# Attention values in a hybrid backbone block: V once in 64 columns of the array, even heads in one half of the columns, odd heads in the other

## The chip, the cores and the metric

The kernel runs on one core of a Trainium2 chip. The metric is the time of one execution on the device in microseconds (us), taken as the median of several runs. The profile is that of one execution; its times are microseconds from its first instruction.

The engines are called PE (matrix products and turns), PEld (the loading of PE's stationary operand), DVE, ACT, POOL (element-wise engines) and SP (here: the queue that issues the loads from memory).

## What is computed

Two layers over 512 latent tokens of width 1024, with 256 context tokens. Each layer is a half-step gated FFN, a token mixer, and a second half-step FFN, all with modulation and normalisation around them. The mixer of the first layer is windowed attention with 16 query heads in 4 groups, one key head and one value head of width 64 for each group. A block of 128 queries sees its own and the neighbouring blocks of keys, all context keys, and a sink logit for each head. The part that matters here:

```python
p = jax.nn.softmax(jnp.concatenate([s_win, s_ctx, sinks], axis=-1), axis=-1).astype(v.dtype)
o = (jnp.einsum('bhgqk,bkhd->bqhgd', p[..., :SPAN], v_b)
     + jnp.einsum('bhgqk,bkhd->bqhgd', p[..., SPAN:SPAN + C_], vc))
```

The mixer of the second layer is a Fourier mixing. All data are float32.

## The kernel before

Weight products are made of three products of rounded float32 parts (`mm3`): weights are loaded (`wr`), cut on ACT (`wh`) and DVE (`wl`), and multiplied. The products of the attention weights with V are plain float32 products.

The stages follow each other: a head, the first FFN over latent tokens, the one over context tokens, the attention (`attention`), its output product (`project` with `attn_wo`), the second FFN, the second layer. Attention first makes K, V and Q in six groups of products (`group`). `kv_post` adds the bias, turns K, and has ACT copy V from `kvb` into a tile of its own, where each value head stands twice side by side: 64 columns and the same 64 columns once more, so that the stationary operand of a value product has 128 columns.

The core of the attention is a loop over 16 steps, a step being a group g and a block b of 128 queries (`steps`). A step has four heads. The order of the instructions on PE, and within the loop on DVE and ACT too, is the order of the program (`pin`). Step n does this:

- `weights_turned(n)`: PE turns the finished attention weights p of the four heads, key tile by key tile (4 key tiles for the first and last block, 5 for the others), into banks `pt`; ACT copies each bank to `pT`, 128 keys by 512 columns (4 heads by 128 queries).
- `scores(n+2)`: PE makes the scores of the step after next into banks `s` (one bank for each head with 4 key tiles, two with 5). DVE adds the mask and takes the running minimum (`nm`), ACT takes the exponentials, DVE adds the sums, takes the reciprocal and scales p.
- In steps 3 to 6 PE turns a part of Q (`q_flip`, banks `qt`), and ACT copies it. From step 7 on, weights of the following output product are gated on DVE and cut on ACT and DVE in between (`gate_next`, `weights`).
- `values(n)`: PE multiplies V by `pT`, one product for each key tile, summed in one bank `o`. Its 128 rows hold the 64 values twice; its 512 columns hold the four heads. From the upper half of the rows ACT copies the even heads to `oT[g]`, from the lower half the odd heads: two copies of 64 rows by 2 heads by 128 queries.

PE has eight banks, given out in the order in which the program asks for them. A bank is free again when its reader has emptied it: ACT for `pt`, `qt` and `o`, DVE for `s`.

After the core, `project` splits `oT` (`uh` on ACT, `ul` on DVE) and PE multiplies it by the cut weights (`y`).

All instructions go through one helper, so that they have the same line, L68, in the profile; they are told apart by the names of their tiles.

Of the kernel before, what the change touches and what calls it, by code (L numbers as in the profile page):

```python
# [10 lines left out]
F32 = mybir.dt.float32  # L11
# [4 lines left out]
P = 128  # L16
# [13 lines left out]
KVH = 4  # L30
GRP = HEADS // KVH
HD = 64
# [68 lines left out]
class Emitter:  # L101
# [33 lines left out]
    def mm(self, out, lhsT, rhs, start, stop):  # L135
        self.nc.tensor.matmul(out, lhsT, rhs, start=start, stop=stop)
# [734 lines left out]
    def attention(self, w_kv, w_q, w_ao, h1, ch, rest):  # L871
        nc = self.nc
        ins = self.ins
        sync = nc.sync
        mm = self.mm
# [13 lines left out]
        V = []  # L889

        def kv_post(tp, ps):
            V.append(self.slot([P, 2, KVH, 2 * HD], F32, "V"))
            kv = self.slot([P, 2, 512], F32, "kvb")
            for tt in range(2):
                nc.vector.tensor_tensor(kv[:, tt], ps[:, tt * 512 : (tt + 1) * 512], bkv, ALU.add)
            kks = []
            for tt in range(2):
                t = 2 * tp + tt
                kr = kv[:, tt, :256]
                if t < NT:  # L900
                    kr = self.rope(kr, tabs[:, 0, t], tabs[:, 1, t], KVH, nc.vector)
                kk2 = self.slot([P, 2, KVH, 2, HD], F32, "kk2")
                k4 = kr.rearrange("p (h d) -> p h d", d=HD)
                for r in range(2):
                    nc.scalar.copy(kk2[:, 0, :, r].bitcast(F32R), k4)
                for r in range(2):
                    nc.vector.tensor_tensor(kk2[:, 1, :, r], k4, kk2[:, 0, :, r], ALU.subtract)
                kks.append(kk2)
            for tt in range(2):
                v4 = kv[:, tt, 256:512].rearrange("p (h d) -> p h d", d=HD).unsqueeze(2)  # L910
                nc.scalar.copy(
                    V[tp][:, tt].rearrange("p h (r d) -> p h r d", r=2), v4.broadcast_to([P, KVH, 2, HD])
                )
            return tp, kks

        def kv_flip(tp, kks, tt):
# [77 lines left out]
        nc.pin(True)  # L994
        ps = group(0, w_kv)
        k0 = kv_post(0, ps)
        flip()
        ps = group(1, w_kv, between=lambda: kv_flip(*k0, 0))
        kv_flip(*k0, 1)
        k1 = kv_post(1, ps)  # L1000
        ps = group(2, w_kv, last=True, between=lambda: kv_flip(*k1, 0))
        kv_flip(*k1, 1)
        bq = self.slot([P, D], F32, "bq")
        sync.dma_start(bq, ins["b_qkv"][:, :D].broadcast_to([P, D]))
        k2 = kv_post(2, ps)
        ps = group(0, w_q[0], between=lambda: kv_flip(*k2, 0))
        kv_flip(*k2, 1)
# [12 lines left out]
        oT = []  # L1020
# [72 lines left out]
        def values(g, b, keys, pT):  # L1093
            nk = len(keys)
            o = self.bank("o")
            for i, kt in enumerate(keys):
                mm(o, V[kt // 2][:, kt % 2, g], pT[i], start=(i == 0), stop=(i == nk - 1))
            tok = slice(b * P, (b + 1) * P)
            for r in range(2):
                rs = slice(r * HD, (r + 1) * HD)  # L1100
                src = o[rs].rearrange("p (c r q) -> p c r q", c=2, r=2)[:, :, r]
                nc.scalar.copy(oT[g][rs, :, tok], src)

        steps = [(g, b) for g in range(KVH) for b in range(NT)]
        oT.append(self.slot([P, 2, SEQ], F32, "oT"))
# [5 lines left out]
        for n, (g, b) in enumerate(steps):  # L1111
            fetch = n >= CORE_FETCH and self.n_split < w_ao + CORE_TILES
            if fetch:
                self.gate_next()
            t = weights_turned(*due.pop(0))
            if b == 0 and g > 0:
                oT.append(self.slot([P, 2, SEQ], F32, "oT"))
            if n + 2 < len(steps):
                due.append(scores(*steps[n + 2]))
            if Q_TURN <= n < Q_TURN + 4:  # L1120
                q_flip(*(q01 if n < Q_TURN + 2 else q11), (n - Q_TURN) % 2)
            if fetch:
                self.weights(self.n_split, ahead=0)
            values(*t)
            if n == 0:
                q11 = q_bias(1, 1, ps1)
                for i in range(4):
                    q_rope(*(q01 if i < 2 else q11), i % 2, nc.gpsimd)
            if Q_TURN - 1 <= n < Q_TURN + 3:
                q_parts(*(q01 if n < Q_TURN + 1 else q11), (n + 1 - Q_TURN) % 2)  # L1130
# [208 lines left out]
```

## Time and profile before

| | us |
|---|---|
| median of three runs | 2053.14 (2052.12 to 2055.15) |
| the profiled execution | 2051.99 |
| its span, first to last instruction | 2050.0 |
| PE busy | 2004.1 |
| weight loads of PE busy | 1684.2 |
| DVE busy | 1324.0 |
| ACT busy | 714.5 |
| the attention core | from about 676 to 811 |

Busy times are shares of the span of one engine each and overlap. A matmul's record in the profile lasts longer than the distance to the next one, since matmuls run in a pipeline; the distance of the starts, or the chain of waits, tells how fast they follow each other. The chain of waits goes back from the last instruction, at each step to what released it or to the instruction before it on its engine.

### The profile page before, as it was taken

The page shows a single profiled execution, that of the slowest core. Times are in us where ns is not written, and L with a number is a line of the kernel's source. Part 1 is how long each engine was busy: PE and PEld are TensorE (multiplying, and loading weights), DVE is VectorE, ACT ScalarE, POOL GpSimd, SP SyncE. Part 2 cuts the span into 40 slices and gives each one's busy share as a digit, 9 for nine tenths or more (in the row PEclk, how much of TensorE's full clock was granted, in tenths as well). Part 3 has the DMA queues.
Part 4 walks back from the last instruction along what each step waited for, and adds up shares of the span by engine and source line. Part 5 has one row for each costly group of instructions (what it writes and reads, how often), then busy time and mean ns, then how long its engine had stood idle before and what let it go on. Part 6 is the DMA issues. An engine that isn't in the chain of part 4 may idle for free.

```text
span 2050.0 us, 25222 instructions
## 1 busy us (share of the span) xinstructions
PE 2004.1 (98%) x9990; PEld 1684.2 (82%) x9990; DVE 1324.0 (65%) x1888; ACT 714.5 (35%) x1090; POOL 50.6 (2%) x56
## 2 busy tenths in 40 slices
PE   6999999999999999999999999999999699999998
PEld 5788888899888776888888888888888688888887
DVE  7659985698756887566558545765764873322754
ACT  3322233433634688322224322222432452222420
POOL 3000000000000300000000000000000000000000
PEclk9999999999999999999999999999999899999999
DMA  9656533387712012365543325654340323332321
GB/s 364 234 197 204 195 125 124 119 314 275 258 48 71 1 42 83 103 225 195 187 164 113 123 95 194 213 196 134 113 144 3 133 92 103 104 102 83 119 76 41
DMA packets 81910, 292.56 MB, mean 143 GB/s; under 512 B 9856, under 2 KB 10112, under 8 KB 81792
## 3 DMA queue, kind: packets, MB, share of 16 engines
q1 hardware_dynamic: 81792, 290.96, 41.4%
q8 instruction: 78, 1.28, 0.3%
q14 instruction: 40, 0.33, 0.0%
HBM read 288.83 MB, written 2.10 MB: 142 GB/s over the span
## 4 chain that ended last, share of the span: by engine, by line
PE 94%; DVE 4%; ACT 1%; issue 0%; DMA 0%; SPq 0%; DVEq 0%; ACTq 0%
PE up L68 52%; PE y L68 31%; PE qkv L68 4%; PE o L68 3%; PE s L68 1%; PE pt L68 1%; DVE acc L68 1%; PE tp L68 1%; DVE p L68 1%; DVE x L68 1%; PE ab L68 0%; PE qt L68 0%; DVE wr L68 0%; DMA wr<-in_wi_head_dram 0%; PE gp L68 0%
## 5 line engine op out<-in xcount | busy, mean ns | idle before, releaser
L68 DVE TENSOR_TENSOR wl<-wr,wh 128x1024 fp32r<-128x1024 f32 x356 | 426.0, 1219 | 108.4 <-ACT wh L68 74.0
L68 ACT CAST wh<-wr 128x1024 fp32r<-128x1024 f32 (+1 forms) x364 | 367.6, 1046 | 189.9 <-PE y L68 85.6
L68 PE MATMUL up<-hh,wh 128*128 128x512 f32 (+1 forms) x1152 | 429.4, 373 | 0.0
L68 PE MATMUL up<-hl,wh 128*128 128x512 f32 (+1 forms) x1152 | 427.9, 371 | 0.0
L68 PE MATMUL up<-hh,wl 128*128 128x512 f32 (+1 forms) x1152 | 427.8, 371 | 0.0
L68 PE MATMUL y<-wh,uh 128*128 128x512 f32 x920 | 303.8, 392 | 13.2 <-ACT X L68 13.2
L68 ACT ACTIVATE sg<-up 128x512 f32<-128x512 f32 (+1 forms) x110 | 61.1, 556 | 715.3 <-PE up L68 715.3
L68 PE MATMUL y<-wh,ul 128*128 128x512 f32 x920 | 302.6, 390 | 0.1
L68 PE MATMUL y<-wl,uh 128*128 128x512 f32 x920 | 302.3, 390 | 0.0
L68 DVE TENSOR_TENSOR u<-up,sg 128x512 f32<-128x512 f32 (+1 forms) x110 | 70.0, 637 | 354.1 <-PE up L68 353.8
L68 PEld LDWEIGHTS up<-hl,wh 128*128 128x128 f32 x1152 | 217.0, 188 | 37.5
L68 PEld LDWEIGHTS up<-hh,wl 128*128 128x128 f32 x1152 | 217.1, 188 | 37.2
L68 PEld LDWEIGHTS up<-hh,wh 128*128 128x128 f32 x1152 | 217.1, 188 | 36.9
L68 PEld LDWEIGHTS y<-wh,uh 128*128 128x128 f32 x920 | 173.4, 189 | 49.5 <-ACT uh L68 13.8
L68 PEld LDWEIGHTS y<-wh,ul 128*128 128x128 f32 x920 | 173.2, 188 | 36.6 <-DVE ul L68 0.6
L68 PEld LDWEIGHTS y<-wl,uh 128*128 128x128 f32 x920 | 173.3, 188 | 35.8
L68 DVE SCALAR_TENSOR_TENSOR acc<-mr,silu_c,acc 128x1024 f32<-128x1024 f32 x147 | 186.0, 1279 | 1.4
L68 PE MATMUL up<-h0h,wh 128*128 128x512 f32 x352 | 139.5, 396 | 3.0 <-ACT h0h L68 3.0
L68 DVE TENSOR_TENSOR wr<-wr,gr 128x1024 f32<-128x1024 f32 x104 | 124.5, 1219 | 22.3 <-DMA wr<-in_wo_dram 20.2
L68 PE MATMUL up<-h0l,wh 128*128 128x512 f32 x352 | 138.3, 393 | 0.0
L68 PE MATMUL up<-h0h,wl 128*128 128x512 f32 x352 | 138.1, 392 | 0.0
L68 DVE SCALAR_TENSOR_TENSOR z<-x,y 128x512 f32<-128x512 f32 x48 | 32.7, 682 | 125.1 <-PE y L68 125.0
(158 smaller groups left out, 2290.7 us busy)
## 6 DMA issues: line engine op xcount, KB each, us to landing
wr<-in_wi_dram SPq DMA_DIRECT2D x213, 512.0 KB, 4.4
mr<-in_mod_w_dram SPq DMA_DIRECT2D x144, 512.0 KB, 4.2
wr<-in_wo_dram SPq DMA_DIRECT2D x110, 512.0 KB, 3.6
m<-in_mod_head_dram SPq DMA_DIRECT2D x16, 512.0 KB, 8.0
wr<-in_wqkv_dram SPq DMA_DIRECT2D x12, 512.0 KB, 3.7
wr<-in_attn_wo_dram SPq DMA_DIRECT2D x8, 512.0 KB, 3.5
wr<-in_fourier_wo_dram SPq DMA_DIRECT2D x8, 512.0 KB, 5.4
wr<-in_wi_head_dram SPq DMA_DIRECT2D x8, 448.0 KB, 9.2
```

The source lines that it names most:

```text
L68: ins = f(*args, **kw)
```

## The change

V is copied once, to 64 columns a head. Each key tile gets two products in place of one: the stationary operand is the same 64 columns of V, the moving operand is the 256 columns of the even heads or of the odd heads, and the result goes to the upper 64 or to the lower 64 rows of the bank, 256 columns wide. ACT then copies the bank to `oT` with one instruction over 128 rows in place of two over 64.

```diff
         def kv_post(tp, ps):
-            V.append(self.slot([P, 2, KVH, 2 * HD], F32, "V"))
+            V.append(self.slot([P, 2, KVH, HD], F32, "V"))
...
             for tt in range(2):
-                v4 = kv[:, tt, 256:512].rearrange("p (h d) -> p h d", d=HD).unsqueeze(2)
-                nc.scalar.copy(
-                    V[tp][:, tt].rearrange("p h (r d) -> p h r d", r=2), v4.broadcast_to([P, KVH, 2, HD])
-                )
+                nc.scalar.copy(V[tp][:, tt], kv[:, tt, 256:512].rearrange("p (h d) -> p h d", d=HD))
...
             o = self.bank("o")
             for i, kt in enumerate(keys):
-                mm(o, V[kt // 2][:, kt % 2, g], pT[i], start=(i == 0), stop=(i == nk - 1))
+                heads = pT[i].rearrange("p (c r q) -> p c r q", c=2, r=2)
+                for r in range(2):
+                    mm(
+                        o[r * HD : (r + 1) * HD, : 2 * P].rearrange("p (c q) -> p c q", c=2),
+                        V[kt // 2][:, kt % 2, g], heads[:, :, r], start=(i == 0), stop=(i == nk - 1),
+                    )
             tok = slice(b * P, (b + 1) * P)
-            for r in range(2):
-                rs = slice(r * HD, (r + 1) * HD)
-                src = o[rs].rearrange("p (c r q) -> p c r q", c=2, r=2)[:, :, r]
-                nc.scalar.copy(oT[g][rs, :, tok], src)
+            nc.scalar.copy(oT[g][:, :, tok], o[:, : 2 * P].rearrange("p (c q) -> p c q", c=2))
```

## Rows read from the trace of the kernel before

**Rows 1.** The page: span, and busy time of each engine with its share.
```profile
span 2050.0 us, 25222 instructions
...
PE 2004.1 (98%) x9990; PEld 1684.2 (82%) x9990; DVE 1324.0 (65%) x1888; ACT 714.5 (35%) x1090; POOL 50.6 (2%) x56
```

**Rows 2.** Busy time by stretch: length, engines (instructions), granted clock, DMA share, GB/s.
```profile
600.00:626.00 26.00, 26.00 (x132) 21.83 (x131) 15.63 (x32) 17.53 (x42) 0.00 (x0) 1.00 0.38 122
...
690.00:740.00 50.00, 50.00 (x280) 36.31 (x279) 42.06 (x131) 40.60 (x106) 6.67 (x7) 1.00 0.04 11
740.00:799.00 59.00, 57.03 (x292) 39.58 (x292) 55.31 (x173) 48.89 (x120) 0.00 (x0) 1.00 0.14 44
799.00:811.00 12.00, 11.87 (x51) 6.98 (x50) 2.85 (x4) 8.29 (x16) 0.00 (x0) 1.00 0.54 183
```

**Rows 3.** DVE's waits, 676 to 811: who, for whom, total, times, longest.
```profile
DVE wl L68 <- ACT wh L68: 9.1, 1, 9.1
DVE p L68 <- PE s L68: 7.3, 4, 2.6
```

**Rows 4.** DVE's timeline, rows with waits: start, length, instruction, [idle before, releaser].
```profile
678.16 0.62 DVE L68 CUSTOM_DVE_ANT_0 p<-s,mask,nsink 128x384 f32<-128x384 f32 x1 [1.49 <-PE s L68]
...
705.00 0.62 DVE L68 CUSTOM_DVE_ANT_0 p<-s,mask,nsink 128x384 f32<-128x384 f32 x1 [1.11 <-PE s L68]
...
731.66 0.75 DVE L68 CUSTOM_DVE_ANT_0 p<-s,mask,nsink 128x512 f32<-128x512 f32 x1 [2.57 <-PE s L68]
...
740.36 0.62 DVE L68 CUSTOM_DVE_ANT_0 p<-s,mask,nsink 128x384 f32<-128x384 f32 x1 [2.15 <-PE s L68]
```

**Rows 5.** Instructions at tile o: ns min/median/max, first and last start, form.
```profile
L68 PEld LDWEIGHTS o<-pT,V x144: 186/190/192, 680.0 to 808.7; 128*128 128x128 f32 x144
L68 PE MATMUL o<-pT,V x144: 590/592/697, 680.0 to 809.2; 128*128 128x512 f32 x144
L68 ACT COPY oT<-o x32: 350/367/373, 685.0 to 810.2; 64x256 f32<-64x256 f32 x32
```

**Rows 6.** The chain of waits: start, length, what, how many.
```profile
690.19 4.29 PE o L68 x10
694.48 2.18 PE pt L68 x20
```

**Rows 7.** Timeline of the weight loads, from scores to values.
```profile
698.29 0.31 PEld L68 LDWEIGHTS o<-pT,V 128*128 128x128 f32 x2
698.84 0.19 PEld L68 LDWEIGHTS o<-pT,V 128*128 128x128 f32 x1 [0.24 <-issue]
```

**Rows 8.** ACT's groups, 560 to 676: busy us, mean ns, idle before.
```profile
L68 ACT COPY V<-kvb 128x512 f32<-128x512 f32 x6 | 3.4, 616 | 0.0
...
L68 ACT CAST K<-kt 128x256 fp32r<-128x256 f32 x16 | 4.8, 385 | 5.4 <-PE kt L68 5.4
```

**Rows 9.** Timeline of SP's queue: the first load of the output weights.
```profile
731.12 0.33 SPq L164 DMA_DIRECT2D wr<-in_attn_wo_dram  x1
```

**Rows 10.** Timelines of ACT, DVE and PE at the core's end.
```profile
798.14 0.75 ACT L68 COPY oT<-o 64x256 f32<-64x256 f32 x2 [0.19 <-PE o L68]
798.91 2.54 ACT L68 COPY pT<-pt 128x512 f32<-128x512 f32 x5
...
805.39 2.05 ACT L68 COPY pT<-pt 128x512 f32<-128x512 f32 x4
807.31 1.08 ACT L68 CAST wh<-wr 128x1024 fp32r<-128x1024 f32 x1
...
809.56 1.22 DVE L68 TENSOR_TENSOR ul<-oT,uh 128x1024 fp32r<-128x1024 f32 x1
...
810.83 0.73 PE L68 MATMUL y<-wh,ul 128*128 128x512 f32 x2
```

**Rows 11.** PE's wait before 688.38; busy time by stretch, as rows 2.
```profile
688.38 0.51 PE L68 MATMUL s<-KC,Q 128*128 128x256 f32 x2 [1.85 <-DVE qb L68]
...
1624.00:1630.00 6.00, 0.00 (x0) 0.00 (x0) 5.93 (x9) 0.08 (x1) 0.00 (x0) 0.50 0.26 79
```

## Prediction

> **What bounds the kernel now.** Busy time first: PE fills 98% of the span [rows 1], so a gain has to shorten PE or a wait of PE. The change touches one stage, the attention core, 676 to 811 us. I read it in pieces, because its limit changes: from 690 to 740 PE is busy all 50 us and DVE 42 of them; from 740 to 799 DVE is busy 55.3 of 59 and PE 57.0; from 799 on DVE has almost nothing left [rows 2]. The reader is to see two engines that are nearly tied. Then DVE's waits: in the whole core it waits 7.3 us for the scores of PE, in four waits, and 9.1 us at the end for ACT's weight cast [rows 3]. So if PE became much faster here, DVE could give back at most these. The timeline of DVE says where: waits of 1.49, 1.11, 2.57 and 2.15 us, the last ending at 740.36 [rows 4]; from there to the last scaling of p no row of DVE shows a wait above 0.2 us, each instruction starting where the one before ends. After 740 PE's speed matters no more until the tail.
>
> **The change, part by part.**
>
> *The products.* A step has 4 or 5 key tiles, 18 for the four blocks of a group, 72 in all. The trace has 144 matmuls and 144 weight loads for them [rows 5], so an f32 product is two loads and two streams. Ten stand in the chain with 4.29 us [rows 6]: 0.429 us each, 144 x 0.429 = 61.8 us of PE. Afterwards each key tile has two products, each of 256 columns: 288 loads and 288 streams. A stream half as long takes 0.215 us, so in series 288 x 0.215 is again 61.8 us; nothing is saved by length. The gain can only come from the two halves streaming side by side. The order is half 0 (two streams), half 1 (two streams), next key tile; started in program order, the second stream of one half can run beside the first of the other, all along the step. Then the 61.8 us become 30.9, some 1.9 us less in a step. No row of before shows a 64-column product, so the price lies between 30.9 and 61.8 us, and above that if loads come out from under the streams (rivals). I take the lower end: the halves share neither columns of the array nor rows of the bank. The Trainium skill, "TensorE: Matmul & The Clock Gate", section "Measured speedup vs the span model", gives 2.38 times for three column tiles; scaled to two that is 1.59 (an estimate from that page), which would make 38.9 us of the 61.8. No run here shows it yet, and DVE sets the end in either case.
>
> *Two changes of array form in each step* (turns, scores and Q turns stay at 128 columns): 32 in all. No row shows one. Bounds: nothing, since a load of another operation already begins behind the running stream without a gap [rows 7]; and 0.35 us, what a stream's record lasts beyond its spacing (592 - 429 = 163 ns) plus an uncovered load (190 ns) [rows 5]. The nearest rows are those of change of operation without a gap, so I take 0.1 us: 3.2 us of PE, which a step with 1.9 us to spare hides. The Trainium skill, "TensorEngine Tiling (Array Packing)", section "Key Properties", says that a change of tiling mode drains the engine; that speaks against the change, and the upper bound above is what a drain would be here, 32 x 0.35 = 11.2 us of PE, still under 30.9.
>
> *ACT's copies of o.* 32 copies of 64x256 at 0.367 us [rows 5] become 16 of 128x256; the copy of that shape out of a bank takes 0.385 [rows 8]. ACT saves 5.6 us over the core, 0.35 in a step. ACT isn't the bound; it counts only in the tail.
>
> *The copies of V*: 6 of 0.616 us become half as wide, about 0.4 (the row of that shape) [rows 8]. They run at 600 to 625 us, while PE is busy 26.0 of 26.0 us [rows 2]; off the path, 0. If that cover were gone they would give 6 x 0.2 = 1.2 us. V's tiles are smaller but remain one slot each, so no load starts earlier through that.
>
> *What follows for DVE, the next limit.* The first wait (678.16) ends before the first product of values: it stays. The other three, 1.11 + 2.57 + 2.15 = 5.83 us [rows 4], are PE arriving late with scores. By 705 PE would have been ahead by half of steps 1 and 2 (20 x 0.215 = 4.3 us), by 731 by 5.6 more, so each is covered by PE's own speed. But PE also can't start scores before ACT has emptied older banks, and ACT follows DVE by the exponentials. Step by step, with five copies of 2.54 us and one of o ahead of them, the banks are free in time for the first two waits and some 0.5 us late for the third (an estimate). So 5.3 us. SP moves along: the first attn_wo load is issued at 731.12 [rows 9], when the core frees a buffer for it, and its gating multiplication stands on DVE between the second and the third wait; its release moves with PE. A load that came late all the same would take the place of the third wait, at most 2.15 us.
>
> *The tail.* Now: ACT copies o(13) at 798.14, pT(14) from 798.91 for 2.54, then waits for PE's o(14), copies pT(15) from 805.39 for 2.05, casts wh at 807.31; DVE's ul starts at 809.56 and y runs unbroken from 810.83 [rows 10]. Afterwards, on the same clock: copy of o(13) from 797.95 to 798.33, pT(14) to 800.87, o(14) ends 0.43 + 0.16 later at 801.5, 16 turns at 2.18/20 = 0.109 us [rows 6] to 803.2, pT(15) to 804.15, wh from 804.1, ul 2.25 after that and y 1.27 after that: 807.6 instead of 810.83, 3.2 us. Next late there is ACT (pT, then wh and uh), no longer PE.
>
> *Sum.* 5.3 + 3.2 = 8.5 us. Behind 811 the order is unchanged and PE-bound, so the shift is carried to the end. The profiled execution took 2051.99 (span 2050.0 and 2.0 around it): 2043.5. The median of the three runs, 2053.14, lies 1.15 above the profiled one: 2044.6.
>
> **The rivals.**
>
> *A. The halves don't overlap* (the change then doesn't do what it is said to): PE keeps 61.8 us and gets 32 changes of form at 0 to 0.35 us, 0 to 11.2. PE is the bound for most of the core, so nearly all of it is paid: 2053 to 2064, at 0.1 us each 2056. For it: no row shows two matmuls at once. Against: the columns and the output rows are disjoint.
>
> *B. Weight loads come out from under the streams; slower.* Loads double to 288. Today a load of 0.19 us starts right as the preceding stream starts and lies within its 0.43 us [rows 7]. The place is inside `values`; if a 64-column load waits for the stream before it, and the halves run in series, an instruction takes 0.215 + 0.095 to 0.19 (half a load to a whole one), 288 x 0.095 to 0.19 = 27 to 55 us more, less some 4 of PE idle in the core: 2076 to 2104, middle 2090. It decides from the point where the exposed part exceeds what the overlap saves, 0.107 us an instruction. The trace speaks against it for 128 columns. The Trainium skill, "TensorE: Matmul & The Clock Gate", section "The mechanism" under packing, has loads overlap running matmuls only where row groups differ, and both halves here use all rows; by that rule this rival would hold. The trace doesn't agree with it in the present form [rows 7].
>
> *C. They overlap, but part is given back*: loads half exposed, or the clock. PE would be idle some 3 to 4 us of a 10 us step after 740. PE's wait of 1.85 us before 688.38 left the core at full clock, 2.4 GHz [rows 2, 11]; after the long idle stretch behind 1618 the granted clock was 0.50, 1.2 GHz [rows 11]. A half clock in part of steps 7 to 12 hides behind DVE, but in the tail turns and values of steps 13 to 15 would take twice as long, and the 3.2 us go, with part of the 5.3: 2047 to 2056, middle 2051.
>
> **How the numbers follow.** Forecast 0.62, with its own range 2041 (ACT's casts ordered better in the tail, the third wait wholly gone) to 2049 (tail without gain, one wait left); A 0.14; B 0.12; C 0.12. A measurement here tells about 0.2%, 4.1 us, from no change. Faster: 0.60 of the forecast and 0.04 of C, 0.64. Same: 0.02 of the forecast, 0.09 of A, 0.06 of C, 0.17. Slower: 0.05 of A, 0.12 of B, 0.02 of C, 0.19. The range from 2041 to 2064 holds forecast, A and C and leaves out B and little else.
>
> **What would show it.** In the profile after: starts of o matmuls of the two halves in pairs, and a step's values in about 2 us instead of 3.4 to 4.3; the three waits of DVE at 705, 731 and 740 gone, and its row of scores waits near 1.5 to 2 us; DVE busy without waits from about 698 to 793; ACT, not PE, ahead of y. Wrong if a step's values still take 3.4 to 4.3 us (A), if they take 5 us and more with idle time of PE before each stream (B), or if the granted clock of the core falls under 1.0 (C).

## The result, and the profile after

The changed kernel takes 2042.14 us (median of four runs, 2041.48 to 2043.41) where the kernel before takes 2052.97 (four runs). The ratio is 0.9947, with a 95% interval from 0.9934 to 0.9959: 10.8 us less, over twice the 0.2% that a measurement tells from no change. The forecast was 2044.6, with 2041 to 2049 as the forecast's own range and 2041 to 2064 as the range that holds two rivals as well; the time lies near the lower end of both. The profiled execution took 2041.51, against 2051.99 before.

The page of the changed kernel. It answers rows 1: PE has 144 more matmuls and is busy 17.3 us less; DVE's work is as long as it was.

```profile
span 2039.7 us, 25478 instructions
...
PE 1986.8 (97%) x10134; PEld 1679.1 (82%) x10134; DVE 1323.7 (65%) x1888; ACT 705.2 (35%) x1074; POOL 50.6 (2%) x56
```

Instructions at tile o, as rows 5: nanoseconds of one (min/median/max), first and last start, form. Twice as many loads and matmuls, each with 64 columns and 256 elements a row; half as many copies, each over all rows and as long as one was.

```profile
L68 PEld LDWEIGHTS o<-pT,V x288: 132/137/231, 679.6 to 798.1; 128*64 128x64 f32 x144
L68 PE MATMUL o<-pT,V x288: 379/379/689, 679.6 to 798.3; 128*64 128x256 f32 x144
L68 ACT COPY oT<-o x16: 350/368/434, 684.6 to 799.4; 128x256 f32<-128x256 f32 x16
```

The chain of waits (start, length, what, how many), as rows 6. Twenty products of values with 5 key tiles take 2.31 us; ten took 4.29. Sixteen with 4 key tiles take 1.90.

```profile
706.21 1.90 PE o L68 x16
...
722.42 2.31 PE o L68 x20
724.73 2.33 PE pt L68 x20
```

PE's timeline, four stretches that all begin at 722.3 and end at 722.45, 722.7, 723.0 and 724.6. What counts is how many matmuls have started by then: two, four, six, and in the end twenty.

```profile
722.35 0.44 PE L68 MATMUL o<-pT,V 128*64 128x256 f32 x2
722.35 0.65 PE L68 MATMUL o<-pT,V 128*64 128x256 f32 x4
722.35 0.87 PE L68 MATMUL o<-pT,V 128*64 128x256 f32 x6
722.35 2.38 PE L68 MATMUL o<-pT,V 128*64 128x256 f32 x20
```

They start in pairs. The single records behind these rows start at 722.349 and 722.356, 722.616 and 722.623, 722.832 and 722.839, then a pair every 0.216 us: one stream of each half of the columns, 7 ns apart. (The records don't name the half; that a pair is one stream of each is inferred here, and the first experiment bears it out.) Two streams of 256 take no longer than one, which takes 0.216 us where it runs alone (first experiment).

The loads of the same step, on the timeline of PEld. Twenty loads of 137 ns are 2.74 us and fit into 1.92: loads lie under the streams, and partly under each other.

```profile
722.35 1.92 PEld L68 LDWEIGHTS o<-pT,V 128*64 128x64 f32 x20 [0.17 <-issue]
724.66 0.14 PEld L68 LDWEIGHTS pt<-ident,p 128*128 128x128 f32 x1 [0.39 <-issue]
```

DVE's waits in the core (who, for whom, total, times, longest), and the places on its timeline that answer rows 3 and 4.

```profile
DVE wl L68 <- ACT wh L68: 5.6, 1, 5.6
DVE p L68 <- PE s L68: 2.1, 3, 1.5
```

```profile
677.75 0.62 DVE L68 CUSTOM_DVE_ANT_0 p<-s,mask,nsink 128x384 f32<-128x384 f32 x1 [1.48 <-PE s L68]
...
697.38 0.75 DVE L68 CUSTOM_DVE_ANT_0 p<-s,mask,nsink 128x512 f32<-128x512 f32 x1 [0.31 <-PE s L68]
...
734.45 0.62 DVE L68 CUSTOM_DVE_ANT_0 p<-s,mask,nsink 128x384 f32<-128x384 f32 x1 [0.31 <-PE s L68]
...
792.12 0.88 DVE L68 TENSOR_SCALAR p<-p,sum 128x512 f32<-128x512 f32 x2
```

The wait ahead of the first product of values stays. The other three, 5.83 us before [rows 4], have become two of 0.31.

The end of the core, as rows 10, on the timelines of ACT, DVE and PE.

```profile
795.57 2.05 ACT L68 COPY pT<-pt 128x512 f32<-128x512 f32 x4 [0.21 <-PE pt L68]
797.48 1.08 ACT L68 CAST wh<-wr 128x1024 fp32r<-128x1024 f32 x1
798.43 1.08 ACT L68 CAST uh<-oT 128x1024 fp32r<-128x1024 f32 x1
```

```profile
799.73 1.22 DVE L68 TENSOR_TENSOR ul<-oT,uh 128x1024 fp32r<-128x1024 f32 x1
```

```profile
799.56 0.73 PE L68 MATMUL y<-wh,uh 128*128 128x512 f32 x2 [0.84 <-ACT uh L68]
801.01 0.74 PE L68 MATMUL y<-wh,ul 128*128 128x512 f32 x2 [0.25 <-DVE ul L68]
```

Where the time went, from the starts of like instructions in both traces:

| | before | after | gained |
|---|---|---|---|
| first row reduction of DVE in the core | 678.16 | 677.75 | 0.41 |
| reduction with the third wait | 740.36 | 734.45 | 5.91 |
| end of the last scaling of p | 799.26 | 793.00 | 6.26 |
| y unbroken | 810.83 | 801.01 | 9.82 |
| span | 2050.0 | 2039.7 | 10.3 |
| profiled execution | 2051.99 | 2041.51 | 10.5 |

The first 0.41 us lie ahead of the core and are not of the change: the stage's first matmul starts at 584.49 before and at 584.08 after, and over the kernels below that agree up to there it starts anywhere from 583.5 to 585.8. For that reason the experiments are read by the stage as well: from the first matmul of the K, V and Q products to the first one of the next FFN, which starts at 856.21 before and at 846.35 after. The stage lasts 271.72 us before and 262.27 after.

The clock did move in the core. Busy time by stretch, columns as rows 2:

```profile
684.00:688.00 4.00, 1.13 (x9) 0.69 (x6) 3.90 (x9) 3.37 (x9) 1.16 (x1) 0.84 0.00 0
688.00:692.00 4.00, 4.00 (x18) 3.35 (x20) 3.80 (x11) 2.69 (x8) 3.89 (x4) 0.50 0.00 0
692.00:696.00 4.00, 4.00 (x30) 2.75 (x27) 3.86 (x8) 1.80 (x6) 3.92 (x5) 0.80 0.00 0
690.00:740.00 50.00, 49.52 (x386) 39.69 (x384) 46.27 (x150) 41.89 (x108) 6.23 (x7) 0.96 0.07 22
740.00:799.00 59.00, 51.58 (x370) 37.66 (x368) 50.95 (x154) 47.09 (x114) 0.00 (x0) 0.94 0.19 61
...
768.00:772.00 4.00, 3.69 (x17) 2.33 (x18) 4.00 (x8) 1.25 (x3) 0.00 (x0) 0.58 0.00 0
...
778.00:782.00 4.00, 4.00 (x16) 2.54 (x18) 3.85 (x10) 2.05 (x4) 0.00 (x0) 0.61 0.00 0
```

PE had waited 2.22 us before 687.95 (1.85 before the change, without effect [rows 2, 11]), and from then to about 693.6 it ran at 1.2 GHz: a granted clock of 0.50 from 688 to 692, and 0.80 as the mean of the next 4 us. The values of that step took 3.65 us for 20 (chain of waits, 690.88) instead of 2.31. DVE paid for it with the 0.31 us at 697.38. That this wait comes from the clock can be seen in the changed kernel run once more (below). There PE waits 2.22 us at the same place, but the clock is low for less of the work behind it (0.72 from 688 to 692, 0.85 from 692 to 696), and of DVE's waits for scores only two are left, the first one and the one at 734:

```profile
688.00:692.00 4.00, 2.35 (x11) 2.35 (x12) 3.91 (x9) 2.17 (x6) 2.27 (x3) 0.72 0.00 0
```

```profile
DVE p L68 <- PE s L68: 1.8, 2, 1.5
```

After 768 and 778 the clock is low again for most of 4 us, behind waits of PE of 1.21 and 1.63 us; there DVE, which has no wait in this stretch, loses nothing.

### The profile page after: what moved, and what is told of

It reads as the page before. It is cut to its first block, busy times and chain, and to the rows that moved or that the text cites. A ratio compares the mean times of both kernels' runs of the same rounds, so it can differ in the third digit from the quotient of the medians.

```text
span 2039.7 us, 25478 instructions
## 1 busy us (share of the span) xinstructions
PE 1986.8 (97%) x10134; PEld 1679.1 (82%) x10134; DVE 1323.7 (65%) x1888; ACT 705.2 (35%) x1074; POOL 50.6 (2%) x56
## 4 chain that ended last, share of the span: by engine, by line
PE 92%; DVE 6%; ACT 1%; issue 1%; DMA 0%; SPq 0%; DVEq 0%; ACTq 0%
PE up L68 52%; PE y L68 31%; PE qkv L68 4%; DVE p L68 2%; DVE acc L68 1%; PE o L68 1%; PE s L68 1%; PE tp L68 1%; PE pt L68 1%; DVE x L68 1%; DVE wr L68 1%; DVE wl L68 0%; PE ab L68 0%; PE qt L68 0%; PE gp L68 0%
```

## The experiments

Ratios are against the kernel before, measured beside each; "the changed kernel" is the one of the result, 0.9947.

### Do the two halves run side by side, and in what order?

Two explanations of the pairs stood against each other. Strict order: PE starts its matmuls in program order, and halves meet only where they are neighbours there. Look-ahead: a matmul for the free half may start ahead of queued ones for the busy half. The first run puts all products of one half before those of the other, so that neighbours share a half.

```diff
-            for i, kt in enumerate(keys):
-                heads = pT[i].rearrange("p (c r q) -> p c r q", c=2, r=2)
-                for r in range(2):
+            for r in range(2):
+                for i, kt in enumerate(keys):
+                    heads = pT[i].rearrange("p (c r q) -> p c r q", c=2, r=2)
                     mm(
```

> All key tiles of the even heads first, then all of the odd heads: the same 288 loads and streams, the same 64 columns, the same merged copies on ACT, but neighbours in the order are of the same half. Theory (the gain is the two halves streaming side by side, started in program order): only one pair of a step can overlap, so a step's values take 19 units of 0.211 us (5 key tiles) or 15 (4), 4.0 and 3.2 us instead of 2.3 and 1.9; the waits of DVE at 705, 731 and 740 come back; 2050 to 2054 us. Rival (the gain comes from ACT's merged copies and from smaller loads, V narrower): it stays at 2042 and the values at 1.9 to 2.4 us.

Measured: 2049.69 us, ratio 0.9981 (0.9971 to 0.9990), 0.3 us under the lower end of what was expected; stage 269.46. Of 9.45 us in the stage 2.26 are left. The chain of waits, PE's timeline (stretches from 724.6 to 725.98, 726.68 and 728.2), and DVE's waits:

```profile
708.88 2.79 PE o L68 x16
...
724.71 3.66 PE o L68 x20
```

```profile
724.64 1.51 PE L68 MATMUL o<-pT,V 128*64 128x256 f32 x6
724.64 2.37 PE L68 MATMUL o<-pT,V 128*64 128x256 f32 x13
724.64 3.73 PE L68 MATMUL o<-pT,V 128*64 128x256 f32 x20
```

```profile
DVE p L68 <- PE s L68: 5.7, 5, 1.7
```

With the same instructions in another order PE is late with scores again, three waits of 0.85, 1.35 and 1.66 us at 706, 731 and 739. So the gain comes from halves that stream at once, and not from shorter copies or a smaller V. But 3.66 and 2.79 us are less than the halves one after the other would take (20 and 16 streams of 0.216, less the overlap of one neighbouring pair, about 4.1 and 3.2). The rows show why: six matmuls have started by 725.98, then seven in the next 0.70 us. In the single records there are two series, each with 0.216 us from start to start behind its first interval (0.267 us). The odd half begins at 725.990, while the even half starts its last four matmuls at 725.984, 726.200, 726.416 and 726.632. The first matmul of the odd half started ahead of three that stand before it in the program.

The second run turns the order of the halves about at every other key tile. In strict order, neighbours of the same half would then follow each other at each tile border and lose a slot there.

```diff
-                for r in range(2):
+                for r in ((0, 1), (1, 0))[i % 2]:
```

> Even, odd for the first key tile, odd, even for the second, and so on: every second boundary lies between two products of the same half. Theory (strictly in order, a stream waits only for its own half): 15 units of 0.211 us for 5 key tiles and 12 for 4, 3.2 and 2.5 us a step; PE is then still ahead of DVE, so the time loses little, 2042 to 2045 us. Rival (the engine picks the streams out of order, or overlaps loads rather than streams): 2.3 and 1.9 us as in the changed kernel, 2042 us.

Measured: 2041.90 us, ratio 0.9944 (0.9929 to 0.9959), as the changed kernel; chain and timeline too:

```profile
722.40 2.31 PE o L68 x20
```

```profile
722.33 2.38 PE L68 MATMUL o<-pT,V 128*64 128x256 f32 x20
```

Strict order falls. The engine looks past queued matmuls of a busy half, by three in these runs.

### What ACT's one copy is worth

The two copies of 64 rows come back; all else stays as changed.

```diff
-            nc.scalar.copy(oT[g][:, :, tok], o[:, : 2 * P].rearrange("p (c q) -> p c q", c=2))
+            for r in range(2):
+                rs = slice(r * HD, (r + 1) * HD)
+                nc.scalar.copy(oT[g][rs, :, tok], o[rs, : 2 * P].rearrange("p (c q) -> p c q", c=2))
```

> The products as changed, but ACT again copies the bank o with two instructions of 64 rows. Theory (DVE sets the pace of the core, ACT only that of the tail): 0.35 us more of ACT in each step, of which the tail pays two to three, 0.7 to 1.1 us, and the waits for ACT's copy of o in steps 7 to 12 grow by 0.35 each without DVE waiting: 2042.5 to 2043.5 us. Rival (the merged copies are what freed the banks sooner and so made the gain): 5 us and more of it go, 2047 us or more.

Measured: 2043.80 us, ratio 0.9953 (0.9938 to 0.9968); stage 263.68, 1.4 us longer; y is unbroken from 802.93 instead of 801.01, and 0.51 of these 1.92 us lie ahead of the stage. The time is 0.3 us above the upper end of what was expected. ACT's share is small. Of the 1.4 us 0.8 lie behind the last scaling of p, in the tail, where ACT has become the last. The other 0.6 lie ahead of it, where PE's waits for the emptied bank of o grow from 6.4 to 7.5 us; two profiles of the changed kernel differ there by 0.4.

### Who sets the pace

Both runs leave out the scaling of p by the reciprocal of its sum: 64 instructions of DVE; without them its busy time on the page of the changed kernel falls from 1323.7 to 1293.4 us, by 30.3. What that gives tells whether DVE or PE was the limit.

```diff
-                for i in range(j, j + 2):
-                    nc.vector.tensor_scalar(s_l[i], s_l[i], sm[:, i : i + 1], None, ALU.mult)
```

On the changed kernel:

> The changed kernel without DVE's scaling of p by the reciprocal sums (left out: the softmax's division; 64 instructions of about 0.5 us, 2 us a step). Theory (DVE sets the pace of the core now): the core gets shorter by much of it, until ACT or PE is next; 2028 to 2036 us. Rival (PE or ACT still sets the pace): under 4 us, 2038 to 2042.

On the kernel before:

> The kernel before, without the same scaling (left out: the softmax's division). Theory (there PE sets the pace up to 740 us and is nearly tied behind it): DVE's relief is worth at most PE's idle time in the core, some 4 us, and the waits of DVE for scores grow: 2048 to 2053 us. Rival (DVE was the bound already): 8 us and more, under 2045.

Measured: 2033.80 us after (ratio 0.9905, 0.9890 to 0.9920) and 2048.90 before (0.9978, 0.9969 to 0.9988), in stages of 253.38 and 267.80. The same relief of DVE is worth 8.9 us of stage after the change and 3.9 before. DVE's waits, after and then before:

```profile
DVE sum L68 <- ACT es L68: 10.8, 15, 1.1
...
DVE p L68 <- PE s L68: 7.3, 5, 2.9
```

```profile
DVE p L68 <- PE s L68: 18.9, 8, 3.7
```

Before, DVE's waits for PE's scores grow by 11.6 us with it (7.3 [rows 3] to 18.9), after by only 5.2 (2.1 to 7.3). Waits for ACT's exponentials, which neither kernel had in these rows, take some 10 us in both. The limit of most of the core has moved from PE to DVE, but not far: of 30.3 us 8.9 reach the end.

### Taking work from DVE that need not lie in the core

DVE also gates and cuts the weights of the output product in steps 7 to 15. Two runs move some of that behind the core: one has four weight tiles ready in it instead of five, the other begins in step 11 instead of 7.

```diff
-CORE_TILES = 5
+CORE_TILES = 4
```

> The changed kernel with 4 instead of 5 tiles of the output weights prepared within the core. Theory (DVE sets the pace of steps 7 to 12, each tile costs it 2.27 us there): the core is shorter by up to 2.3 us; the tile then has to be made beside the output product, where DVE is busy for the first 20 us as well, so that PE may wait there: 2040 to 2042.5 us. Rival (DVE has room in the core): no change in the core, 2042 or more.

```diff
-CORE_FETCH = 7
+CORE_FETCH = 11
```

> The changed kernel with the preparation of output weights beginning at step 11 instead of 7, so that part of it falls into steps 14 and 15, where DVE has no scores. Theory (DVE is the bound up to step 13 and idle behind it): steps 7 to 10 lose 2.3 us each, steps 14 and 15 hide two tiles: up to 4.5 us off the core, less one or two casts of 0.95 us that come into ACT's chain of the tail: 2038 to 2041 us. Rival (ACT's chain in the tail takes all of it): 2042 to 2044.

Measured: 2043.54 (ratio 0.9954, 0.9942 to 0.9967) and 2042.16 (0.9943, 0.9931 to 0.9956). Neither is faster than the changed kernel; both expectations missed. (The five runs with four tiles lie apart, from 2042.38 to 2046.49, so that their median says little.) Counted from the first score, the last value product starts 2.4 us sooner with four tiles and 5.0 us sooner with the late weights, so the relief of DVE does reach PE. But 1.5 and 1.7 us of that go at once into a longer wait for ACT's `uh` ahead of y, the loss that the rival of the late weights had named. In the second the core is still shorter, from the first score to y 136.92 us instead of 140.20, but from y to the next FFN it took 49.83 instead of 46.80. PE's timeline, and busy time by stretch:

```profile
796.09 1.22 PE L68 MATMUL y<-wh,uh 128*128 128x512 f32 x2 [2.57 <-ACT uh L68]
797.11 1.05 PE L68 MATMUL y<-wl,uh 128*128 128x512 f32 x2
798.59 1.22 PE L68 MATMUL y<-wh,ul 128*128 128x512 f32 x2 [0.43 <-DVE ul L68]
```

```profile
796.00:800.00 4.00, 3.48 (x7) 2.32 (x8) 4.00 (x5) 1.38 (x3) 0.00 (x0) 0.51 0.41 98
```

PE waits 2.57 us for ACT's `uh`, where it waited 0.84 in the changed kernel, and then its first products of y run at a granted clock of 0.51, two in 1.22 us instead of 0.73. With four tiles the wait is 2.36 us and the granted clock from 796 to 804 is 0.79. The suspicion: what is left of DVE's gain, the clock takes back. The next run keeps the late weights and has PE multiply K with itself ten times while it would wait; the products are not used.

```diff
+        filler = self.bank("fill")
+        for _ in range(10):
+            mm(filler, KX[0][:, 0, :P], KX[0][:, 0], start=True, stop=True)
         nc.pin(False)
```

> The kernel of the run with the weights late in the core, and 10 products of K with itself (their result is read by nobody) behind the last values, where PE waited 2.57 us there. Theory (that run's earlier start of the output product, 3.5 us, was given back because PE's wait dropped its clock to 1.2 GHz for the first 6.9 us of the output product): with PE kept busy the granted clock stays at 1.00 there, the first y products take 0.73 us a pair instead of 1.22, and some 2 us are gained: 2039.5 to 2041 us. Rival (the gain went to DVE, which has no time for the rest of the weights): 2042 and clock or no clock the same.

Measured: 2038.99 us, ratio 0.9927 (0.9914 to 0.9941), 3.2 us below the run without the filler and 0.5 below what was expected; all five executions are faster than all five without it. From y to the next FFN it takes 47.83.

```profile
792.64 2.56 PE L68 MATMUL fill<-K 128*128 128x512 f32 x10
795.16 0.73 PE L68 MATMUL y<-wh,uh 128*128 128x512 f32 x2
...
797.66 0.73 PE L68 MATMUL y<-wh,ul 128*128 128x512 f32 x2 [1.31 <-DVE ul L68]
```

```profile
796.00:800.00 4.00, 2.69 (x12) 1.98 (x11) 3.96 (x5) 1.65 (x3) 0.00 (x0) 1.00 0.60 165
```

The stage is 2.7 us shorter (259.32 instead of 262.02), 2.0 of it behind the first y, where the clock is 1.00 instead of 0.51. So unused work in the place of the wait does gain time, and the clock is what it gains by behind y. Of the other 0.7 us 0.43 are a wait of DVE for scores at 697.33, which the profile without the filler has and this one has not; the filler stands behind that place, so this part is not its doing. The rival, that DVE has no time for the rest of the weights, is there in part: PE now waits 1.31 us for DVE's `ul`, which stands behind weights on DVE, and from y on it still takes 1.0 us more than in the changed kernel.

### A better version

Better than filler is no wait. Half of `oT` is finished when group 1 ends, and can be split long before the core does. ACT casts `uh` of it in step 11 and DVE makes `ul` in step 13; `project` then uses these.

```diff
+            if n == EARLY_CAST:
+                self.first = (self.slot([P, 2, SEQ], F32R, "uh"), self.slot([P, 2, SEQ], F32R, "ul"))
+                nc.scalar.copy(self.first[0], oT[0])
+            if n == len(steps) - 3:
+                nc.vector.tensor_tensor(self.first[1], oT[0], self.first[0].bitcast(F32), ALU.subtract)
...
-        rest = self.project(w_ao, KC, self.halves_of(oT, SEQ, KC), st, NT)
+        rest = self.project(w_ao, KC, self.halves_of(oT, SEQ, KC, {0: self.first}), st, NT)
...
-    def halves_of(self, us, N, count=NF):
+    def halves_of(self, us, N, count=NF, cache=None):
...
-        cache = {}
+        cache = {} if cache is None else cache
...
+EARLY_CAST = 11
```

It was run alone and with the late weights, and beside them the changed kernel once more.

> The changed kernel once more, for the comparison within these runs: 2041 to 2043.5 us.

> The changed kernel with the first split of oT (one ACT cast, one DVE subtraction) put into steps 11 and 13 of the core, in place of behind the last copy of the core. Theory (behind the last values the path runs through ACT's casts wh and uh and DVE's ul, 2.3 us from the end of the values to the unbroken output product): y starts right behind the values, 1.5 to 2.5 us sooner: 2039.5 to 2041 us. Rival (the cast in step 11 delays ACT's chain by as much): 2041.5 to 2043 us.

> Both: the first split of oT inside the core and the weights beginning at step 11. Theory: the values end some 5 us sooner than in the changed kernel and y starts right behind them, at full clock; DVE then has all the remaining weights beside the output product, which may hold PE up there: 2037 to 2040 us. Rival (DVE's load beside the output product takes it back): 2041 us or more.

Measured: the changed kernel again 2041.78 (ratio 0.9943, 0.9930 to 0.9955); the early split 2040.45 (0.9937, 0.9925 to 0.9950); both edits 2036.56 (0.9915, 0.9902 to 0.9929), 0.4 below what was expected and the fastest version that computes the whole of it. PE's timeline of the last one:

```profile
792.55 2.12 PE L69 MATMUL o<-pT,V 128*64 128x256 f32 x16 [0.57 <-ACT pT L69]
794.60 0.73 PE L69 MATMUL y<-wh,uh 128*128 128x512 f32 x2
795.16 0.63 PE L69 MATMUL y<-wl,uh 128*128 128x512 f32 x2
```

y follows the last value product without a wait, and at full clock. The early split alone is worth 1.3 us, which five runs each don't separate well, the late weights alone nothing, and both 5.2: one needs the other. The early split takes away the two waits of PE that the late weights had brought, for ACT's `uh` (2.57 us) and, with the filler, for DVE's `ul` (1.31 us); which of the two counts for more was not tried. The last run asks whether they would have been worth as much without the change.

> The kernel before (128 columns of V) with the two edits of the run of both: first split of oT inside the core, weights from step 11. Theory (there PE sets the pace of the core, so relief of DVE in steps 7 to 10 buys nothing, and only the way from the last values to the unbroken output product, 1.5 us, is saved): 2050.5 to 2052.5 us. Rival (the two edits are worth 5 us whatever the products): 2048 us or less.

Measured: 2050.08 us, ratio 0.9986 (0.9977 to 0.9995), 3.1 us below the kernel before; the expectation, from 2050.5 us on, is missed by 0.4. DVE there waits for scores again:

```profile
DVE p L69 <- PE s L69: 13.0, 7, 3.3
```

PE has these 13.0 us still ahead of DVE, so a lighter DVE helps less there. The two edits give 5.2 us with the change and 3.1 without; the difference of 2 us points the same way but lies within the intervals of the two ratios.

## Why the prediction held, step by step

**The products.** Taken at 30.9 us for all 144 old products. A group of four blocks now takes 1.90 + 2.31 + 2.31 + 1.90 = 8.42 us in the chain at full clock, four groups 33.7, with the changes of form in it, instead of 61.8. In pairs the gain is 0.429 / 0.216 = 1.99, over a step 4.29 / 2.31 = 1.86. The Trainium skill, "TensorE: Matmul & The Clock Gate", section "Measured speedup vs the span model", scaled to two tiles gave an estimate of 1.59; the traces do not agree, they show more. One detail of this step failed: "started in program order". The turned order and the halves in series show that a matmul of the free half passes queued ones. Here it changed nothing, since the order was the good one anyway.

**Changes of array form.** Taken at 0.1 us each. A step of 20 products takes 2.31 us in the chain where ten pairs are 2.16: 0.15 us. The turns behind it take 2.33 instead of 2.18 [rows 6]: 0.15 again. So 32 x 0.15 = 4.8 us of PE instead of 3.2, within the bound of 11.2 and, up to the tail, hidden behind DVE. The loads show it too. Before, the first turn's load came 0.24 us after the last load of values, under the last stream:

```profile
702.27 0.14 PEld L68 LDWEIGHTS pt<-ident,p 128*128 128x128 f32 x1 [0.24 <-PE o L68]
```

Now it comes 0.39 us after it, at 724.66, when the last pair (724.343 and its 0.216 us) is over. That agrees with the Trainium skill, "TensorEngine Tiling (Array Packing)", section "Key Properties", that a change of tiling mode drains the engine; the drain is small here.

**DVE's waits.** 5.3 us were expected, 5.83 less 0.5 at the third. Measured: 5.83 - 0.31 - 0.31 = 5.2. The 0.31 at 734.45 is the late start that was estimated at 0.5. The one at 697.38 was not foreseen; it is the low clock from 688 on. That the sum still meets 5.3 is partly luck: in the second profile of the changed kernel that wait is absent and the sum would be 5.5. That DVE bounds the core from there on is shown by the runs without scaling.

**The tail.** 3.2 us expected. From the end of the last scaling to unbroken y it took 810.83 - 799.26 = 11.57 before and 801.01 - 793.00 = 8.01 after: 3.56. The order of events is as worked out, ACT now being ahead of y, with a wait of PE of 0.84 us.

**ACT's copies and those of V.** 32 x 0.367 = 11.7 us became 16 x 0.368 = 5.9: 5.9 less, expected 5.6. The copies of V went to 401 ns, expected about 0.4, and moved nothing: from the first K, V and Q product to the first score it takes 75.28 us before and after.

**The sum.** 8.5 us against 10.5 in the profiled executions. The waits gave 5.2 and the tail 3.56; 0.41 is the head, which is not of the change and is chance; about 0.3 up to 734 and 0.35 from there to 793 are DVE's instructions following each other a little closer, and 0.5 to 0.7 lie behind y and outside the span. What was left out of the sum is small, and none of it was tested.

**The rivals.** A (no overlap) fell with the pairs. B (loads exposed) fell with the twenty loads in 1.92 us. Its rule from the Trainium skill, "TensorE: Matmul & The Clock Gate", section "The mechanism", that loads overlap running matmuls only where row groups differ, does not hold here: all loads use all rows and lie under streams, in the present and in the new form. C named the right danger in the wrong place. The clock did fall, in three stretches of some 4 us, but not in the tail, so that only 0.31 us of it was paid. Of the prediction's own signs of being wrong, the one for C did come true: the granted clock of the core fell under 1.0, to 0.96 from 690 to 740 and 0.94 from 740 to 799. The sign was too coarse, since C's times needed the fall in the tail; the two falls in the later steps hid behind DVE, as C itself had said of such falls. The wait of 1.85 us that had left the clock at full [rows 2, 11] was no measure of a safe one either: falls came behind waits of 1.21 and 1.63. The late weights bring C about in the tail, with 2 to 3 us.

## What to carry to other kernels

Two products that each need half of the array's columns and write to different rows are worth issuing as one interleaved pair, if the engine they free is the limit: here they took half the time, but of the 28 us won on PE some 9 reached the end, and the next engine's waits in the same stretch [rows 3, 4] told most of that beforehand. Where an edit frees time behind PE and the total doesn't move, read the granted clock after PE's new wait before blaming the edit. Moving the wait's cause (an early split of half of the operand) gave more than the edit alone.

## What the runs showed of the hardware

- Two f32 matmuls of 64 columns with all 128 rows start 7 ns apart and a pair follows every 0.216 us, as long as one stream of 256 takes alone (724.905 to 725.121 in the run with the halves in series).
- A matmul for a free half of the columns started ahead of three queued ones for the busy half (725.990 against 726.200, 726.416 and 726.632).
- A change between 128 and 64 columns cost 0.15 us each way.
- The granted clock fell from 2.4 to 1.2 GHz behind waits of PE of 1.21, 1.63, 2.22 and 2.57 us, and did not behind others of 1.13, 1.25 and, before the change, 1.85 us. The length of a single wait doesn't tell the cases apart: in the second profile of the changed kernel the same wait, 1.22 us before 768.34, left the clock at 1.00, and so did one of 2.49 us before 787.15 in the run with the late weights. What does tell them apart was not tried. With ten unused matmuls in the place of the wait of 2.57 us the clock stayed at 1.00.
